# S5 rotations and input matrices in the down projection's buffers, z split in round 5, eight temporaries, a new order table

## The chip, the cores and the metric

The kernel runs on one core of one Trainium2 chip. The metric is device time in microseconds of one launch. The kernel before takes 1371.43 us, the median of three runs (1370.65 to 1372.84).

## The reference, cut to what matters

One layer of a hybrid decoder, for 1024 prompt positions and 8 x 4 sample positions, which stand side by side as 1056 columns (NT). All is float32.

```
proj   = x @ w_in                          # x_lru | u_s5 | two gates
h_lru  = rg_lru(conv4(x_lru))              # gated linear recurrence, 1024 channels
y_s5   = s5_ssm(u_s5)                      # complex diagonal state space, 32 groups of 16 channels, 64 states
z      = gelu(y_s5);  glu = z @ w_glu
merged = sigmoid(g_lru) * h_lru + sigmoid(g_s5) * glu_a * sigmoid(glu_b)
x1     = layer_norm(ALPHA * x + merged @ w_out)
up     = x1 @ w_up                         # 2 x 3072
f      = (gelu(conv3(up_a)) * up_b) @ w_down
y      = layer_norm(ALPHA * x1 + f)
```

The states after the last position are returned too.

## The kernel before, in words

Each large product is taken in three passes. A float32 tensor is split into a high part (rounded by ScalarE, `scopy`) and the rest (subtracted on VectorE, `tt`); TensorE adds hi*hi, hi*lo and lo*hi in PSUM. So each weight tile costs one load (`wx`), one ScalarE cast (`wh`) and one VectorE subtraction (`wl`), all of 128x1024.

The program has these stages. First come four tiles of the input projection for S5 (PSUM tiles `psu`), with the parameters of S5 worked out beside them in a long chain of small VectorE operations (`s5_params`, line 705). Then eight rounds j follow (line 1104). A round has three products of 72 matmuls of 352 columns each: the RG-LRU input (`psx`), the RG-LRU gate (`psl`) and the S5 gate (`psg`); then the recurrence of one block of 128 channels (`lru_rec`), whose two gate products are six small groups of three matmuls (`psr`). Beside them, S5 runs in four batches ut: `s5_consts(ut)` (step c, line 809) makes the batch's tables and `s5_batch(ut)` (step b, line 881) runs it; `z_split` (step z, line 1075) splits the result for the next product. PLAN says in which round each of these stands in the written program. The GLU product (`psab`), the output projection (`pso`) with the first layer norm, the up projection (`ps`) and the down projection (`pd`) with the second layer norm follow. The last two use a scheme of seven products in place of eight, which needs sums of weight tiles: `s_prep(q)` (line 1409) loads four tiles of w_down (`spx`, `spy`, `spz`, `spv`), forms four sums on VectorE and stores them to DRAM (`s`) for the down projection, for q from 0 to 5.

In S5 the names are: `par` holds the parameters, `tmc` products of them, `CA` the output matrices, `bk` the input vectors laid out for a product `psk`, `BA` and its transpose `BT` (through PSUM, `pst`) the input matrices, `F` the rotations, `U` the input, `V` its image (`psv`), `G` the scanned states, `H` the states turned back, `psy` the output, and `zs` its place in DRAM.

Buffers are rings: a tile takes the slot that comes free first, and its first writer waits for that. The ring "w" has ten slots of 1024 numbers for weights; in the kernel before it also serves `F` and `BT` (INW, line 306). The ring "p" has three slots (NPREP, line 242); in the kernel before its users are `s_prep` and later the input pieces of the down projection. The ring "e" has seven temporaries, "m" six small ones.

The order is set by a planner that runs when the program is built (`schedule`, line 144). Each recorded operation has a priority: its place in the written program less the sum of the boosts of its labels (DEFAULT and BOOST). The planner steps through time with a cost for each operation, and gives an engine the ready operation of the best priority among those that could start soonest. The tiles of one ring are taken in the order of the written program. All loads and stores are issued by SyncE, one after another. Each engine then runs its own list in order on the chip; an instruction that waits holds back all that stand behind it on its engine.

Of the kernel before, what the change touches and what calls it, by code (L numbers as in the profile page):

```python
# [8 lines left out]
F32 = mybir.dt.float32  # L9
# [60 lines left out]
class Program:  # L70
# [173 lines left out]
SPREP = {4: 0, 7: 1, 10: 2, 13: 3, 16: 4, 19: 5}  # L244
NWT_SLOT = 10
LOOK = 2
NSLOT, NTEMP, NMID = 28, 7, 6
PE1 = [0, 0, 0, 1]
PE2 = [0, 4, 0, 0]
SPL = (1,)  # L250
BACC = {"dynamic_dma_scratch_size": 1024}
PLAN = {0: "c0 b0 c1", 1: "b1 c2", 2: "b2 c3", 3: "b3", 4: "z0 z1 z2 z3"}
DEFAULT = {"df": 200, "dw": 200, "l": -100, "w": 300, "wa": 300, "wu": 300, "s": 200, "e": 150}
BOOST = {
# [34 lines left out]
}  # L289
WCUT = [slice(0, 256), slice(256, 512), slice(512, 1024)]  # L290
XCUT = 2
# [11 lines left out]
LACT = 'b'  # L303
G1 = [2, 2, 2, 2]
G2 = [4, 1, 4, 4]
INW = {"F", "BT"}


def build(tc, ins, outs):
# [103 lines left out]
    with ExitStack() as st_:  # L413
# [6 lines left out]
        def slot(shape, dt=F32, name="sl"):  # L420
            return pr.tile(up, shape, dt, "u", NSLOT, name)
# [10 lines left out]
        def wslot(shape, dt=F32, name="wt"):  # L432
            return pr.tile(wp, shape, dt, "w", NWT_SLOT, name)
# [3 lines left out]

        def sslot(shape, name):
            key = name.rstrip("0123456789")
            return wslot(shape, F32, name) if key in INW else slot(shape, F32, name)  # L440

        def fixed(shape, name, dt=F32):
            return pr.tile(cp, shape, dt, name, 1, name)
# [213 lines left out]
        par = slot([1088], name="par")  # L657
# [309 lines left out]
        def lru_in(j):  # L967
            psx = mmps(f"psx{j}")
            gemm(psx, wtile(lgpos(0, j)), xs)
            xp = temp([1083], name=f"xp{j}")  # L970
            gset(xp[:, 0:3], 0.0)
            xq = xp[:, 1027:1083].rearrange("p (b q) -> p b q", q=7)
            with boosted("e"), boosted("ex"):
                for c in range(NCH):
                    n = CH if c < 2 else 320
                    scopy(xp[:, 3 + CH * c:3 + CH * c + n], psx[c][:, :n])
                scopy(xq[:, :, 3:7], psx[2][:, 320:352].rearrange("p (b q) -> p b q", q=4))
            gcopy(xq[:, :, 0:3], lh[:, j])
            gcopy(olru[:, j, 0:3], xp[:, 1024:1027])
            gcopy(olru[:, j, 3:27].rearrange("p (b q) -> p b q", b=NB), xq[:, :, 4:7])  # L980
            xc = temp([LL], name=f"xc{j}")
            with boosted(f"cv{j}"):
                act(xc[:, :], xp[:, 3:3 + LL], AF.Identity, bias=cv("cb")[:, j:j + 1], scale=cw[:, 3, j:j + 1])
                for k in range(3):
                    stt(xc[:, :], xp[:, k:k + LL], cw[:, k, j:j + 1], xc[:, :], MUL, ADD)
            return xc

        def lru_gate(j):
            psl = mmps(f"psl{j}")
            gemm(psl, wtile(lgpos(1, j)), xs)  # L990
            gg = temp([NT], name=f"gg{j}")
            with boosted("e"), boosted("egl"):
                for c in range(NCH):
                    act(gg[:, CH * c:CH * c + CH], psl[c][:, :CH], AF.Sigmoid)
            return gg
# [102 lines left out]
        u_tile(3)  # L1098
        cs = {}
        plan = PLAN  # L1100
        cur = lru_in(0), lru_gate(0)
        if GWPOS == 0:
            lru_weights(0)
        for j in range(NK):
            nxt = None
            if GWPOS == 1:
                lru_weights(j)
            if j + 1 < NK:
                if GWPOS == 0:
                    lru_weights(j + 1)  # L1110
                with boosted(f"in{j + 1}"):
                    xc = lru_in(j + 1)
                with boosted(f"lg{j + 1}"):
                    nxt = xc, lru_gate(j + 1)
            with boosted(f"gs{j}"):
                s5_gate(j)
            for w in plan.get(j, "").split():
                q = int(w[1])
                with boosted(f"s{j}"), boosted(w):
                    if w[0] == "c":  # L1120
                        cs[q] = s5_consts(q)
                    elif w[0] == "b":
                        s5_batch(q, cs.pop(q))
                    else:
                        z_split(q)
            if GWPOS == 2:
                lru_weights(j)
            lru_rec(j, *cur)
            cur = nxt
        dma(outs["o_lru"], olru)  # L1130
        dma(outs["o_s5"], os5)
# [537 lines left out]
```

## Time and profile before

| what | before |
|---|---|
| median of three runs | 1371.43 us |
| the profiled execution's own time | 1372.17 us |
| its span | 1370.4 us |
| TensorE matmul busy | 1332.7 us |
| VectorE busy | 1084.0 us |
| ScalarE busy | 599.3 us |
| granted TensorE clock, mean | 0.99 |

The span runs from the first to the last instruction of the profiled execution; the launch's own time is 1.8 us longer. A matmul's record overlaps that of the next, so a busy TensorE says only that it never stood still; how fast it went is read from the number of matmuls in a stretch and the time of that stretch. "Idle before" names who released the engine.

### The profile page before, as it was taken

What the parts mean: (1) busy time and instruction counts of PE and PEld (TensorE: products, weight loads), DVE (VectorE), ACT (ScalarE), POOL (GpSimd) and SP (SyncE); (2) the same over time, 40 slices, a digit from 0 to 9 for tenths busy, and PEclk for the clock granted to TensorE, in tenths of its full rate; (3) what the DMA queues carried; (4) which work ended last, traced back from release to release, by engine and by line L of the source; (5) the groups of instructions that cost most, each with busy time, mean ns of one, the idle gap of its engine ahead of it and who ended that gap; (6) DMA issues with size and microseconds to landing.
All of it is one profiled execution on the core that took longest, in us unless ns stands there. A gap on an engine that the chain in (4) does not pass through costs nothing.

```text
span 1370.4 us, 24666 instructions
## 1 busy us (share of the span) xinstructions
PE 1332.7 (97%) x10040; PEld 1319.6 (96%) x10040; DVE 1084.0 (79%) x1825; ACT 599.3 (44%) x800; POOL 70.2 (5%) x184
## 2 busy tenths in 40 slices
PE   8999988999999999999999999999999999999995
PEld 8999888899999999999999999999999999999995
DVE  6989998896589865779999788888788875555895
ACT  6422625657678332455333333333332443433463
POOL 0000011010011000000010000000000000000000
PEclk9999998999999999999999999999999999999997
DMA  9856744434223651142343322332222387864251
GB/s 333 270 173 228 220 139 110 105 100 153 77 79 127 239 191 47 65 126 93 105 137 127 118 94 103 110 110 87 94 102 87 133 318 292 307 204 158 65 204 64
DMA packets 89330, 201.88 MB, mean 147 GB/s; under 512 B 11008, under 2 KB 40832, under 8 KB 89216
## 3 DMA queue, kind: packets, MB, share of 16 engines
q1 hardware_dynamic: 89216, 200.30, 43.7%
q8 instruction: 79, 1.29, 0.4%
q14 instruction: 35, 0.29, 0.1%
HBM read 142.17 MB, written 58.09 MB: 146 GB/s over the span
## 4 chain that ended last, share of the span: by engine, by line
PE 87%; DVE 7%; issue 2%; ACT 1%; DMA 1%; SPq 1%; DVEq 0%; ACTq 0%
PE ps L395 35%; PE pd L395 18%; PE pso L395 7%; PE psab L395 7%; PE psg L395 5%; PE psl L395 4%; PE psx L395 4%; PE psu L395 4%; PE psr L395 2%; DVE tmc L327 1%; DVE tm L327 1%; SPq L374 1%; DVE xc L339 1%; PE psy L395 1%; DMA wx<-wall 1%
## 5 line engine op out<-in xcount | busy, mean ns | idle before, releaser
L395 PE MATMUL pd<-fh,dh 128*128 128x264 f32 x672 | 192.3, 286 | 0.0
L395 PE MATMUL pd<-fh,dl 128*128 128x264 f32 x672 | 191.3, 285 | 0.0
L395 PE MATMUL pd<-fl,dh 128*128 128x264 f32 x672 | 190.9, 284 | 0.0
L395 PEld LDWEIGHTS pd<-fl,dh 128*128 128x128 f32 x672 | 126.5, 188 | 0.2
L395 PEld LDWEIGHTS pd<-fh,dh 128*128 128x128 f32 x672 | 126.4, 188 | 0.2
L395 PEld LDWEIGHTS pd<-fh,dl 128*128 128x128 f32 x672 | 126.6, 188 | 0.0
L327 DVE TENSOR_TENSOR dl<-dx,dh 128x1024 fp32r<-128x1024 f32 x48 | 58.1, 1220 | 48.8 <-ACT dh L364 44.2
L395 PE MATMUL pso<-mm,wh 128*128 128x264 f32 x512 | 95.4, 287 | 0.0
L364 ACT CAST dh<-dx 128x1024 fp32r<-128x1024 f32 x48 | 49.8, 1049 | 81.0 <-PE pd L395 71.3
L339 DVE SCALAR_TENSOR_TENSOR ac<-fx,con,ac 128x1072 f32<-128x1072 f32 x48 | 64.0, 1333 | 25.9 <-ACT ac L360 25.3
L395 PEld LDWEIGHTS pso<-mm,wh 128*128 128x128 f32 x512 | 79.9, 188 | 0.5
L364 ACT CAST wsh<-wa 128x1024 fp32r<-128x1024 f32 x24 | 25.2, 1051 | 122.7 <-DVE wa L327 113.2
L395 PE MATMUL pso<-mm,wl 128*128 128x264 f32 x256 | 72.7, 284 | 0.0
L327 DVE TENSOR_TENSOR wl<-wx,wh 128x1024 fp32r<-128x1024 f32 (+2 forms) x48 | 54.1, 1130 | 16.7 <-ACT wh L364 10.5
L395 PE MATMUL psg<-xh,wh 128*128 128x352 f32 x192 | 63.8, 332 | 3.5 <-ACT wh L364 3.5
L395 PE MATMUL psg<-xh,wl 128*128 128x352 f32 x192 | 63.2, 329 | 1.5 <-DVE wl L327 1.5
L364 ACT CAST wh<-wx 128x1024 fp32r<-128x1024 f32 (+2 forms) x48 | 46.8, 976 | 40.8 <-DMA wx<-wall 34.8
L395 PE MATMUL psab<-zh,wl 128*128 128x352 f32 (+1 forms) x200 | 63.4, 317 | 0.0
L395 PE MATMUL psab<-zh,wh 128*128 128x352 f32 (+1 forms) x200 | 63.4, 317 | 0.0
L395 PE MATMUL psab<-zl,wh 128*128 128x352 f32 (+1 forms) x200 | 63.1, 316 | 0.0
L395 PE MATMUL psg<-xl,wh 128*128 128x352 f32 x192 | 63.1, 328 | 0.0
L395 PE MATMUL psl<-xh,wh 128*128 128x352 f32 x192 | 62.6, 326 | 0.0
(321 smaller groups left out, 4570.0 us busy)
## 6 DMA issues: line engine op xcount, KB each, us to landing
f<-gt SPq DMA_DIRECT2D x84, 264.0 KB, 2.1
wx<-wall SPq DMA_DIRECT2D x42, 512.0 KB, 4.6
fr<-f SPq DMA_DIRECT2D x30, 528.0 KB, 5.5
wa<-wall SPq DMA_DIRECT2D x29, 512.0 KB, 4.4
wg<-wall SPq DMA_DIRECT2D x24, 512.0 KB, 3.6
dx<-wall SPq DMA_DIRECT2D x24, 512.0 KB, 4.4
dx<-s SPq DMA_DIRECT2D x24, 512.0 KB, 6.3
fr<-f SPq DMA_DIRECT2D x24, 264.0 KB, 3.3
```

The costliest lines, as they stand in the source:

```text
L327: pr.add("DVE", 69 + 1.0417 * fsize(out), lambda: V.tensor_tensor(out=out, in0=a, in1=b, op=op), [a, b], [out])
L339: lambda: V.scalar_tensor_tensor(out=out, in0=a, scalar=sc, in1=b, op0=op0, op1=op1),
L364: pr.add("ACT", (51 if psum(a) else 93) + 0.8333 * fsize(out), lambda: S.copy(out, a), [a], [out])
L374: pr.add("SP", fsize(x) * x.ap[0][1] * 4 / 320.0, lambda: nc.sync.dma_start(out, a), [a], [out])
L395: T.matmul(o, lhsT=l, rhs=r, start=st, stop=sp, skip_group_check=skip)
```

## The change

`F` and `BT` are now taken from the ring "p" by `prep` (INP). In the written program S5 stands ahead of `s_prep`, so "p" now serves the eight tiles of S5 first, then the 24 of `s_prep`, then the down projection's input pieces. The ring "w" holds weights alone. There are eight temporaries in place of seven and five small ones in place of six. The four z splits stand in round 5 of the plan, not 4. The whole table of boosts is new. A new function `s5_steps` holds the loop over a round's S5 steps; a plan may now name steps behind the recurrence (after a "|"), but this plan has none.

```
-NSLOT, NTEMP, NMID = 28, 7, 6
+NSLOT, NTEMP, NMID = 28, 8, 5
-PLAN = {0: "c0 b0 c1", 1: "b1 c2", 2: "b2 c3", 3: "b3", 4: "z0 z1 z2 z3"}
+PLAN = {0: "c0 b0 c1", 1: "b1 c2", 2: "b2 c3", 3: "b3", 5: "z0 z1 z2 z3"}
 BOOST = {
...
-    "gs4": 31, "gs5": 3401, "gs7": 68, "in2": 499, "in3": 128, "in4": 1996, "in5": -36, "in7": -11, "l20": 1043,
...
+    "s3": 5923, "s4": 61, "s5": 564, "sp0": -1857, "sp1": 1911, "sp2": 105, "sp4": 297, "sp5": 55, "ue0": 18,
...
-INW = {"F", "BT"}
+INW = set()
+INP = {"F", "BT"}
...
         def sslot(shape, name):
             key = name.rstrip("0123456789")
-            return wslot(shape, F32, name) if key in INW else slot(shape, F32, name)
+            return (wslot if key in INW else slot)(shape, F32, name) if key not in INP else prep(shape, name)
...
+        def s5_steps(steps, j):
+            for w in steps.split():
+                q = int(w[1])
+                with boosted(f"s{j}"), boosted(w):
+                    if w[0] == "c":
+                        cs[q] = s5_consts(q)
+                    elif w[0] == "b":
+                        s5_batch(q, cs.pop(q))
+                    else:
+                        z_split(q)
...
-            for w in plan.get(j, "").split():
...
+            before, _, after = plan.get(j, "").partition("|")
+            s5_steps(before, j)
             if GWPOS == 2:
                 lru_weights(j)
             lru_rec(j, *cur)
+            s5_steps(after, j)
             cur = nxt
```

What the new table does to the order is shown at three places; the names end in the tiles' own numbers.

SyncE near the start, before: the first DMAs behind the load of the third weight tile (`wx_149`); `scs` is the block of S5 parameters.

```order
L374 DMA wx_149<-wall 128x1024
L374 DMA spx_1028<-wall 128x1024
L374 DMA spy_1029<-wall 128x1024
L374 DMA spz_1030<-wall 128x1024
L374 DMA wgx_181<-wgate 128x256
L374 DMA scs<-scon 128x1072
L374 DMA sbc<-scon 128x1024
```

The same place of the kernel after:

```order
L375 DMA wx_149<-wall 128x1024
L375 DMA wgx_184<-wgate 128x256
L375 DMA scs<-scon 128x1072
L375 DMA sbc<-scon 128x1024
L375 DMA wx_152<-wall 128x1024
L375 DMA wx_155<-wall 128x1024
```

The loads of `s_prep` have left this place. The first of them now stands behind the loads of the fourth batch's tables, two rows ahead of a weight tile of round 6 (`wx_480`), and the last of the 24 stores just ahead of the loads for the first layer norm.

VectorE where S5's first tables are made, before: from the first `CA` to the last `bk` of batch 0.

```order
L327 TENSOR_TENSOR CA_210<-tmc_209 64x512 x2
L339 SCALAR_TENSOR_TENSOR xc_173<-xp_172,con,xc_173 128x1080
L327 TENSOR_TENSOR tmc_209<-sbc,par 128x512 x2
L339 SCALAR_TENSOR_TENSOR CA_210<-tmc_209 64x512 x2
...
L327 TENSOR_TENSOR wl_192<-wx_190,wh_191 128x1024
L327 TENSOR_TENSOR tb<-sbc,tmp 128x256
L327 TENSOR_TENSOR spv_1116<-spv_1116,spz_1115 128x1024
L327 TENSOR_TENSOR par<-tb 128x256
L327 TENSOR_TENSOR wl_200<-wx_198,wh_199 128x1024
L343 COPY bk_211<-par 64x4x16 x2
```

The same place of the kernel after:

```order
L328 TENSOR_TENSOR CA_210<-tmc_209 64x512 x2
L328 TENSOR_TENSOR tb<-sbc,tmp 128x256
L328 TENSOR_TENSOR tmc_209<-sbc,par 128x512 x2
L328 TENSOR_TENSOR par<-tb 128x256
L340 SCALAR_TENSOR_TENSOR CA_210<-tmc_209 64x512 x2
L344 COPY bk_211<-par 64x4x16 x2
L328 TENSOR_TENSOR tmc_209<-par 128x512
```

The `spv` sum, the weights' subtractions and the three convolution steps `xc` have left the stretch. On TensorE the product that needs `CA` and `bk`, `psk_212`, has moved with them: before it stood behind the second of the three parts of round 1's `psx`, after 480 matmuls; now it stands straight behind round 0's `psx`, after 360.

TensorE at the first recurrence (`psr`), before: one row of each group is shown.

```order
L395 MATMUL psr_0_0_248<-xch_245,wgh_182 128x360
...
L395 MATMUL psr_0_1_249<-xch_245,wgh_182 128x360
...
L395 MATMUL psr_0_2_250<-xch_245,wgh_182 128x360
...
L395 MATMUL psr_1_0_252<-xch_245,wgh_182 128x360
...
L395 MATMUL psr_1_1_253<-xch_245,wgh_182 128x360
...
L395 MATMUL psg_0_276<-xh_80,wh_265 128x352
```

The same place of the kernel after:

```order
L396 MATMUL psr_0_1_249<-xch_245,wgh_182 128x360
...
L396 MATMUL psx_0_261<-xh_80,wh_199 128x352
...
L396 MATMUL psr_0_2_250<-xch_245,wgh_182 128x360
...
L396 MATMUL psr_1_0_252<-xch_245,wgh_182 128x360
...
L396 MATMUL psx_1_262<-xh_80,wh_199 128x352
...
L396 MATMUL psr_1_1_253<-xch_245,wgh_182 128x360
```

The six groups stood one behind another; now 24 matmuls of a wide product stand between each two pairs. The recurrences of rounds 1 and 2 were taken apart in the same way. From the output projection on, TensorE's list is the same but for a few swaps of neighbouring groups, and its last 60 rows are the same row for row.

## Rows read from the trace of the kernel before

**Rows 1.** The page: span; busy us (share) and instructions of two engines.
```profile
span 1370.4 us, 24666 instructions
...
PE 1332.7 (97%) x10040; PEld 1319.6 (96%) x10040; DVE 1084.0 (79%) x1825; ACT 599.3 (44%) x800; POOL 70.2 (5%) x184
```

**Rows 2.** Busy time by stretch: from:to, length, engines, granted clock, DMA share, GB/s.
```profile
100.00:200.00 100.00, 95.85 (x670) 92.47 (x669) 94.76 (x158) 38.50 (x63) 8.76 (x21) 1.00 0.62 199
200.00:250.00 50.00, 42.92 (x269) 39.85 (x265) 44.53 (x80) 26.67 (x38) 6.00 (x12) 0.86 0.35 87
...
280.00:400.00 120.00, 120.00 (x757) 120.00 (x756) 81.70 (x94) 76.93 (x102) 11.25 (x20) 1.00 0.32 103
400.00:510.00 110.00, 110.00 (x708) 110.00 (x708) 90.35 (x107) 61.36 (x90) 8.59 (x9) 1.00 0.54 178
...
660.00:1285.00 625.00, 625.00 (x5126) 624.92 (x5125) 483.72 (x783) 221.10 (x244) 26.25 (x88) 1.00 0.42 147
```

**Rows 3.** The chain that ended last: start us, us, what.
```profile
54.78 11.57 PE psx L395 x72
...
204.70 0.64 PE pst L399 x4
...
252.47 1.85 PE psk L395 x29
...
274.38 1.08 PE psv L395 x16
...
298.81 2.78 PE psy L395 x24
...
359.46 1.00 PE psr L395 x6
...
412.66 1.92 PE psab L395 x12
...
434.95 75.44 PE psab L395 x492
510.40 26.27 PE pso L395 x216
```

**Rows 4.** The same chain inside 200 to 280 us.
```profile
207.88 3.21 PE psr L395 x9
...
217.59 6.10 PE psg L395 x22
...
264.80 0.77 PE psr L395 x3
265.60 0.57 ACT gt L360
```

**Rows 5.** VectorE from 50 to 280 us by form: count, busy us, mean ns.
```profile
L327 DVE TENSOR_TENSOR wl<-wx,wh 128x1024 fp32r<-128x1024 f32 x14 | 17.0, 1217 | 5.1 <-ACT wh L364 5.1
...
L327 DVE TENSOR_TENSOR spz<-spy,spz 128x1024 f32<-128x1024 f32 x5 | 6.1, 1219 | 0.0
```

**Rows 6.** VectorE's timeline from 54 to 90 us: start, us, instruction.
```profile
56.26 1.22 DVE L327 TENSOR_TENSOR spy<-spx,spy 128x1024 f32<-128x1024 f32 x1
...
66.04 1.28 DVE L327 TENSOR_TENSOR tmc<-sbc,par 128x512 f32<-128x512 f32 x2
...
69.83 1.34 DVE L339 SCALAR_TENSOR_TENSOR xc<-xp,con,xc 128x1080 f32<-128x1080 f32 x1
71.09 1.28 DVE L327 TENSOR_TENSOR tmc<-sbc,par 128x512 f32<-128x512 f32 x2
...
82.49 1.23 DVE L327 TENSOR_TENSOR wl<-wx,wh 128x1024 fp32r<-128x1024 f32 x1 [3.06 <-ACT wh L364]
...
85.89 0.41 DVE L343 COPY bk<-par 64x64 f32<-64x64 f32 x2
```

**Rows 7.** ScalarE's timeline from 30 to 42 us: the sines of S5.
```profile
38.08 0.32 ACT L360 ACTIVATE tmp<-tmp 128x16 f32<-128x16 f32 x2
```

**Rows 8.** TensorE's waits over the span: waited for, us in total, times, longest.
```profile
PE psg L395 <- ACT wh L364: 3.5, 2, 3.2
...
PE ps L395 <- ACT fx L364: 1.4, 1, 1.4
```

More of the change, by code (lines that the diff above doesn't have):

```diff
@@ L1116, in build @@
                 s5_gate(j)
-            for w in plan.get(j, "").split():
[L1118 to L1125, printed above, removed]
+            before, _, after = plan.get(j, "").partition("|")
+            s5_steps(before, j)
             if GWPOS == 2:
```

66 rows, old and new, of the table BOOST are left out of this document.

## Prediction

> **What bounds the kernel now.** I read the page's first part, then busy time by stretch, then the chain that ended last, then VectorE's forms and timeline. By the page TensorE is busy 1332.7 of 1370.4 us [rows 1]. From 660 to 1285 us, and from 280 to 510, it never stands still [rows 2], so whatever is gained ahead of 280 us is handed on whole, as long as nothing else falls late. The place to look at is 50 to 280 us, where TensorE has gaps and VectorE is busy 94.76 us of 100 [rows 2].
>
> What TensorE loses there I take by counting its work from the first `psx` to the first `pso`, that is from 54.78 to 510.40 us, 455.6 us [rows 3], at the pace of undisturbed pieces. Eight rounds of three products of 72 matmuls at 11.57 us are 277.7. The 144 `psr` at 1.00/6 us are 24.0. Of 600 `psab` 492 take 75.44, and the other 108 at 1.92/12 take 17.3. S5's float32 matmuls show as two records each: 128 `psk` at 1.85/29 us (8.2), 128 `psv` at 1.08/16 (8.6), 128 `psy` at 2.78/24 (14.8); with 32 transposes at 0.64/4 (5.1) the sum is 431.1 us [rows 3]. So 24.5 us are lost, all of it ahead of 280 us. Part of it is the clock: nine `psr` took 3.21 us where 1.50 are due, and 22 `psg` 6.10 where 3.5 are due, 4.3 us together [rows 4]; the mean granted clock of that stretch is 0.86 [rows 2], so the engine ran part of it at 1.2 GHz and the rest at 2.4, after waits around the transposes at 204.70 and the `psr` at 207.88 us [rows 3, 4]. Part is the six `psr` groups in a row: three matmuls take 0.77 us, then a ScalarE step of 0.57 us must free one of two PSUM banks [rows 4]. The largest named wait, 3.2 us of `psg` for a cast [rows 8], is also of this stretch. The rest is waiting for S5's tables.
>
> **The sums of `s_prep` leave the front.** Of the 24 sums 20 run between 50 and 280 us: four forms of five, 6.1 us each, 24.4 us [rows 5]. None feeds anything before the down projection. They go because `F` and `BT` hold "p" until S5 is through. The planner had put them into short pauses of chains; on the chip a sum of 1.22 us in a pause of some tenths pushes the chain back by most of its length. Started behind one another such operations cost 1.14 us (1.22 less the 0.08 by which the records of two neighbours overlap, as 69.83 and 71.09 show for an operation of 1.34 [rows 6]). Taken whole that is 22.8 us of VectorE time that the front no longer carries, against 24.5 us lost: of the right size, but not one for one, because the order of TensorE changes too.
>
> **S5 starts earlier, and waits at its start.** `psk` of batch 0 stands 120 matmuls earlier, so TensorE reaches it at 54.78 + 11.57 = 66.4 us. When is VectorE ready? Before, 28.0 us pass from the sines (38.08) to the first `tmc` (66.04) [rows 6, 7]. Four sums lie in it (the `spy` at 56.26 is one), 4.6 us; without them 23.4 remain, and as many weight subtractions stand there as before. The sines come at most 1 us sooner: S5's parameters no longer queue behind 1.5 MB of `s_prep` on SyncE, but the sines stand behind copies of `psu` on ScalarE, which TensorE sets. That gives 60.5 us. From the first `tmc` to the last `bk` 20.3 us pass before [rows 6]; three `xc` at 1.26, three weight subtractions and one sum at 1.14 and the wait of 3.06 us leave the stretch, 11.4 us, so 8.9 remain: 69.4 us. TensorE waits 3 us. The next such place is `pst`: 2.0 us of `psk` and 48 matmuls (7.7) later, at 79.1 us, it needs `BA`, which VectorE has after three `xc`, one subtraction, four operations like `tmc`, and small ones, about 11 us, so at 80.4 and for the second half 2 us later than TensorE could use it: 2 us. By the same count `psy` of batch 0 just fits, `psk` of batch 1 waits 1.3 us, and I leave 2 us for what I can't see: 8.3 in all. From there VectorE is ahead: with its list priced by the means of its forms and TensorE's by its pace, the tables of batches 1 and 2 stand 7 to 37 us further ahead of their users than before. Queued behind the wait at `psk` on TensorE are `psl` of round 0 and all else, so the wait counts in full. Bounds: if the chain from the sines does not shorten, 5 us more; if VectorE's list runs without pauses, all but 2 us vanish. I keep 2 to 14 and take 8.
>
> **The `psr` groups are taken apart.** With 24 matmuls (3.9 us) between pairs, 0.57 us of ScalarE is covered; if the cover is gone, 0.7 us a group comes back, 8 us for batches 0 to 2 at most. This and the clock are inside the 24.5 us.
>
> **What comes later.** The 20 sums, their 20 loads and 20 stores go to 280 to 510 us, where VectorE is busy 81.70 + 90.35 = 172 us of 230 [rows 2]: with 24.4 us it is at 85%. Batch 3 also moves 169 rows back on TensorE (27 us), so some 13 us of its VectorE work falls here too: 91%. Loads and stores, 20 MB, add 90 GB/s to 103 and 178; at 0.54 of the DMA engines for 178 GB/s this reaches 0.8. I cost it at nothing, covered by the 9% and by DMA queues that are not full; the bound is the second rival. The z splits a round later, the small ring at five and 51 table loads on ScalarE where 46 stood (76.93 us of 120 busy) have room. The ring "w" with all ten slots lets weights come earlier, which is in the vanishing 3.2 us wait. The start and the tail don't change: the first loads carry the same bytes ahead of the first matmul, and the last TensorE rows are the same. The 1.4 us at `ps` [rows 8] I leave.
>
> **Sum.** 24.5 - 8 = 16.5 us gained. From the profiled execution's own 1372.2 us that is 1355.7; the median of the runs lies 0.7 lower, so 1355 us.
>
> **Rivals.** First, the clock. The waits at 66 and 79 us lie among float32 `psk` and transposes, as the waits before the slow stretch did [rows 3, 4]. If the clock falls again, 4.3 us come back by [rows 4]: 1359. The Trainium skill, TensorE: Matmul & The Clock Gate, section on a second failure mode, says that short idles between groups that cycle through PSUM banks can swing the clock between its levels. This trace agrees at 200 to 250 us, and shows full clock in 100 to 200 us despite 4.2 us without matmuls [rows 2], so I give it 13%.
>
> Second, slower. VectorE falls late between 400 and 510 us. At 91% the stretch is as dense as 100 to 200 us was, and a sum whose load is late holds all behind it, the merges (`mm`) too, for which `pso` waits. If the loss per us is that of before (24.5 us in 230), the same 24.5 us are lost again, and with the 8 us at the start the kernel stands at 1372 + 8 = 1380. It decides from the point at which VectorE's pauses exceed 9% there. For it speaks that the last sum stands only 16 operations ahead of the last merge in VectorE's list; against it that at 82% (90.35 of 110 us) TensorE lost nothing there [rows 2]. 11%.
>
> Third, nothing. The loss was S5's own latency, not VectorE's load, and comes back in the new order at other places: 1369. The Trainium skill, Perfetto Trace Analysis, on identifying the most-contended engine, would name TensorE by the whole run, and then a change that takes no matmul away gives nothing; its passage on several regimes in one kernel says the opposite, and the stretches of [rows 2] show two regimes. 12%.
>
> **How the numbers follow.** The forecast (gain 10 to 23 us) has 61%, the clock 13%, nothing 12% (half within 0.2%, which is 2.7 us and about what a measurement of this kernel can tell), slower 11%, and 3% for more than 23 us. The likeliest case alone spans 1349 to 1362. For 8 in 10 I take 1345, which is nearly all of the loss and the 1.4 us regained, to 1368. Faster 0.83, same 0.06, slower 0.11.
>
> **What would show it.** In the profile after, the first `pso` should start near 494 us, not 510. TensorE's waits should name `psk` for `bk` and `pst` for `BA` with 2 to 4 us each between 66 and 82 us, and little from 120 to 280. No sum should stand ahead of 280 us, the granted clock of 200 to 250 us should be 1.00, and `psr` should wait for no `gt`. I am wrong if TensorE loses over 3 us between 280 and 510 us, or if the waits ahead of 120 us exceed 14 us.

## The result and the profile after

The kernel after takes 1353.03 us, the median of four runs (1352.81 to 1353.98); the kernel before took 1372.13 us beside it (1370.65 to 1373.48). The ratio is 0.986, with a 95% interval of 0.9845 to 0.9879, a gain of 19 us. Forecast were 1355 us and a range of 1345 to 1368.

The page of the kernel after answers to [rows 1]:

```profile
span 1351.0 us, 24674 instructions
...
PE 1326.4 (98%) x10040; PEld 1318.4 (98%) x10040; DVE 1080.8 (80%) x1825; ACT 603.9 (45%) x805; POOL 79.8 (6%) x184
```

The work is the same. TensorE's busy time is only 6 us less, which says little, since a matmul's record overlaps that of the next. The stretches of [rows 2] in the kernel after (columns as there; its last stretch ends 19 us sooner):

```profile
100.00:200.00 100.00, 100.00 (x702) 98.78 (x701) 78.39 (x134) 49.37 (x73) 10.21 (x23) 1.00 0.36 92
200.00:250.00 50.00, 49.29 (x330) 48.17 (x329) 39.23 (x64) 26.72 (x38) 5.60 (x11) 1.00 0.20 65
280.00:400.00 120.00, 118.90 (x764) 118.05 (x765) 103.02 (x115) 81.02 (x108) 21.83 (x20) 1.00 0.73 245
400.00:510.00 110.00, 110.00 (x740) 110.00 (x739) 100.49 (x128) 58.55 (x86) 8.19 (x9) 1.00 0.76 254
660.00:1266.00 606.00, 606.00 (x4969) 605.93 (x4968) 464.95 (x750) 214.48 (x238) 24.47 (x84) 1.00 0.43 149
```

From 200 to 250 us 330 matmul records stand where 269 stood, and the clock is 1.00, not 0.86. VectorE falls from 94.76 to 78.39 us of 100 in the front, and rises from 172 to 203.5 us of 230 behind it. The last stretch is full in both.

Where the time went is read from two starts. The `psx` and `pso` products of the kernel after (instruction form and count; shortest, median, longest ns; first and last start in us):

```profile
L396 PE MATMUL psx<-xh,wh x192: 317/323/431, 54.9 to 354.5; 128*128 128x352 f32 x192
L396 PE MATMUL pso<-mm,wh x512: 278/284/483, 492.0 to 589.4; 128*128 128x264 f32 x171
```

From the first to the other 437.1 us pass, where 455.6 passed before [rows 3]: 18.5 of the 19 us are gained between them. TensorE's waits in the kernel after from 54 to 520 us are few (us in total, times, longest):

```profile
PE psk L396 <- DVE bk L344: 2.0, 1, 2.0
PE psv L396 <- ACT V L365: 1.6, 2, 1.1
PE psv L396 <- issue: 0.2, 1, 0.2
```

The 3.5 us of `psg` for `wh` [rows 8] are gone, and no wait of `psr` or `pst` is listed. The 1.4 us of `ps` for `fx` [rows 8], behind this stretch, are gone too. The chain that ended last shows the start of S5 in the kernel after (start, us, what):

```profile
59.97 1.17 DVE tmc L328 x2
...
68.27 0.20 DVE bk L344
...
68.60 2.25 PE psk L396 x29
70.85 9.09 PE psl L396 x48
79.94 0.87 PE pst L400 x8
```

`tmc` stood at 66.04 us before, and the last `bk` at 85.89 [rows 6]. The 48 `psl` take 9.09 us where 7.7 are due (48/72 of 11.57), and the 29 `psk` 2.25 where 1.85 are due [rows 3], because the clock falls behind the wait for `bk`. The granted clock is the third number from the end of a stretch's row; from 70 to 74 us it is 0.58:

```profile
70.00:74.00 4.00, 4.00 (x24) 3.94 (x20) 3.90 (x11) 2.48 (x3) 0.45 (x3) 0.58 0.01 3
```

All 24 sums now run between 299 and 479 us. One of their four forms in the kernel after, from 280 to 510 us, as in [rows 5]:

```profile
L328 DVE TENSOR_TENSOR spz<-spy,spz 128x1024 f32<-128x1024 f32 x6 | 7.3, 1216 | 0.1
```

### The profile page after: what moved, and what is told of

It reads as the page before. It is cut to its first block, busy times and chain, and to the rows that moved or that the text cites. A ratio compares the mean times of both kernels' runs of the same rounds, so it can differ in the third digit from the quotient of the medians.

```text
span 1351.0 us, 24674 instructions
## 1 busy us (share of the span) xinstructions
PE 1326.4 (98%) x10040; PEld 1318.4 (98%) x10040; DVE 1080.8 (80%) x1825; ACT 603.9 (45%) x805; POOL 79.8 (6%) x184
## 4 chain that ended last, share of the span: by engine, by line
PE 93%; DVE 3%; ACT 2%; DMA 1%; issue 1%; SPq 0%; ACTq 0%; DVEq 0%
PE ps L396 36%; PE pd L396 18%; PE pso L396 7%; PE psab L396 7%; PE psg L396 7%; PE psl L396 6%; PE psx L396 5%; PE psu L396 2%; PE psr L396 1%; PE psy L396 1%; DVE tmp L328 1%; DMA wx<-wall 1%; PE psk L396 1%; PE psv L396 0%; DVE par L328 0%
## 5 line engine op out<-in xcount | busy, mean ns | idle before, releaser
L340 DVE SCALAR_TENSOR_TENSOR ac<-fx,con,ac 128x1072 f32<-128x1072 f32 x48 | 64.0, 1333 | 24.5 <-ACT ac L361 23.7
L365 ACT CAST wh<-wx 128x1024 fp32r<-128x1024 f32 (+2 forms) x48 | 47.1, 982 | 38.0 <-DMA wx<-wall 23.6
L361 ACT ACTIVATE ac<-fx,con 128x1072 f32<-128x1072 f32 x24 | 30.8, 1285 | 74.4 <-DVE fx L328 65.4
L396 PE MATMUL psl<-xl,wh 128*128 128x352 f32 x192 | 62.5, 326 | 0.0
```

The source lines that it names most:

```text
L340: lambda: V.scalar_tensor_tensor(out=out, in0=a, scalar=sc, in1=b, op0=op0, op1=op1),
L361: pr.add("ACT", c, lambda: S.activation(out=out, in_=a, func=f, bias=bias, scale=scale), [a] + [x for x in (bias, scale) if isap(x)], [out ...
L365: pr.add("ACT", (51 if psum(a) else 93) + 0.8333 * fsize(out), lambda: S.copy(out, a), [a], [out])
L396: T.matmul(o, lhsT=l, rhs=r, start=st, stop=sp, skip_group_check=skip)
```

## The experiments

The theory to test (A) was the prediction's: the sums' VectorE time in the front is the loss. Its rivals were that TensorE's order is what counts (B), and that the new table is (C).

For each kernel the table gives the time that TensorE loses between the first `psx` and the first `pso`. The starts of all its products stand in the trace; from the time to the next start I take what the same product takes undisturbed (the fastest fifth of its kind in the kernel after), and what is left over is lost. Some 5 us of each row are small steps between kinds of products, so the rows are to be compared with each other. The orders differ, so the cut is made by work done and not by time: "front" is the first 210 us of work, which end at 273 us in the kernel after; "behind" is the rest. "To before" is the ratio to the kernel before, run beside it, with its interval.

| kernel | median us | to before | front lost | behind lost |
|---|---|---|---|---|
| before | 1372.1 | | 29.1 | 0.5 |
| after | 1353.0 | 0.9862 (0.9845-0.9879) | 8.1 | 2.8 |
| 1 before, sums late | 1387.3 | 1.0101 (1.0086-1.0116) | 25.8 | 18.9 |
| 2 after, 20 extra operations | 1367.7 | 0.9961 (0.9948-0.9974) | 24.1 | 3.0 |
| 3 before, ring alone | 1400.1 | 1.0195 (1.0180-1.0210) | 8.9 | 48.6 |
| 4 after, ring undone | 1391.7 | 1.0136 (1.0119-1.0153) | 43.4 | 7.4 |
| 5 after, `psr` in a row | 1356.6 | 0.9887 (0.9871-0.9904) | 10.7 | 5.3 |
| 6 after, z in round 4 | 1371.8 | 0.9998 (0.9988-1.0007) | 8.0 | 23.6 |
| 7 before, all but the table | 1386.7 | 1.0108 (1.0092-1.0123) | 10.6 | 34.7 |
| 8 after, three small moves | 1353.8 | 0.9865 (0.9851-0.9880) | 9.5 | 3.5 |
| 9 before, weights early | 1390.5 | 1.0128 (1.0113-1.0143) | 30.7 | 19.6 |
| 10 after, start shifted | 1353.0 | 0.9854 (0.9838-0.9871) | 7.7 | 2.8 |
| 11 after, sizes undone | 1382.9 | 1.0077 (1.0061-1.0093) | 7.7 | 32.8 |
| 12 run 9, one reader early | 1391.0 | 1.0131 (1.0109-1.0154) | 30.3 | 16.7 |

**1. The sums alone.** The order that the planner made is kept, and only `s_prep` is moved in it (the list of places, BEHIND, is left out here).

```
+        order = self.schedule()
+        moved = {i for v in BEHIND.values() for i in v}     # the 72 operations of s_prep
+        for i in order:
+            if i not in moved:
+                for k in (i, *BEHIND.get(i, ())):
+                    self.ops[k][2]()
```

> The kernel before with its own order, sizes, rings and table; only the 72 operations of `s_prep` (24 loads, 24 sums, 24 stores) are taken out of the planned order and put back about where the kernel after has them (none ahead of 280 us). TensorE's list stays the old one: `psk` of batch 0 behind 480 matmuls, `psr` groups in a row. Theory A (the sums' VectorE time in the front is the loss, in whichever order): of the loss ahead of 280 us the waits for S5's tables between 196 and 224 us (about 12 us with the half clock behind them) go, the `psr` groups in a row keep some 6 us: 1354 to 1361 us. Theory B (the loss is TensorE's order: S5's products too late and `psr` in a row; VectorE's time was hidden): 1368 to 1373 us, nothing gained.

VectorE did become free where the sums had stood, up to 193 us. From 100 to 150 us it is busy 35.28 us of 50, where it was 47.50 before. From 200 to 250 us, where no sum stood, it is as busy as before (44.08 against 44.53), and the granted clock is 0.83, no better than the 0.86 of before:

```profile
100.00:150.00 50.00, 49.79 (x360) 48.59 (x359) 35.28 (x75) 15.24 (x29) 1.01 (x6) 1.00 0.21 53
...
200.00:250.00 50.00, 44.24 (x254) 41.24 (x254) 44.08 (x78) 26.06 (x38) 6.03 (x13) 0.83 0.31 85
```

The front won 3.3 us of 29.1. TensorE's waits no longer name `bk`, `CA` or `BA`, but the others stayed, and the half clock with them (from 54 to 520 us; of the 3.5 us of `psr` for `gt` 2.1 lie ahead of 280 us):

```profile
PE psr L409 <- ACT gt L374: 3.5, 8, 0.9
PE psg L409 <- ACT wh L378: 3.2, 2, 3.0
...
PE pst L413 <- DVE F L357: 1.4, 1, 1.4
PE pst L413 <- ACT xch L378: 1.3, 1, 1.3
```

So theory A falls for the old order: 22.8 us of VectorE's time taken away give 3.3. And with the same 72 operations the stretch behind loses 18.4 us more, where the kernel after loses 2.3 more. Theory B did not foresee that either: it said 1368 to 1373. Which of the waits behind the front the moved operations cause was not taken apart.

**2. VectorE's time alone, in the new order.**

```
         for i in self.schedule():
             self.ops[i][2]()
+            if i in EXTRA:
+                self.extra()
...
+        full = con[:, 0:960].rearrange("p (a b) -> p a b", a=16)
+        pr.extra = lambda: V.tensor_reduce(out=dum[:, :], in_=full, axis=AX.X, op=ADD)
```

> The kernel after with 20 extra VectorE operations of about a sum's length (a reduction of 128x960) put into VectorE's list at the times at which the 20 sums stood before, from 56 to 191 us; nothing waits for them, no DMA goes with them, and TensorE's order is the new one. Theory A (VectorE's time in the front counts): most of 20 x 1.1 = 22 us comes back, 1363 to 1375 us, with TensorE waiting for `bk`, `BA` and the tables of batches 1 and 2. Theory B (the new order of TensorE brought the gain): 1353 to 1357 us.

The extra operations from 50 to 200 us by form (the twentieth starts at 208.0 us), TensorE's waits from 54 to 300 us, and its stretch from 183 to 192 us:

```profile
L472 DVE TENSOR_REDUCE dum<-con 128x16 f32<-128x960 f32 x19 | 21.7, 1142 | 0.0
```

```profile
PE psk L401 <- DVE bk L349: 5.0, 1, 5.0
PE psy L401 <- POOL H L373: 4.9, 2, 3.9
PE psk L401 <- DVE CA L345: 3.1, 2, 2.8
```

```profile
183.00:192.00 9.00, 6.58 (x31) 6.58 (x32) 8.62 (x20) 3.35 (x4) 1.48 (x2) 0.62 0.33 111
```

14.7 us come back for some 22 us of VectorE's time (16.0 in the table's count). 11.0 of these 16.0 us are waits for S5's tables and states, 13.0 in the three rows where the kernel after has 2.0. The other 5 are lower clock behind such waits, as in the last row (0.62). In the new order theory A holds; theory B falls. The two runs together: neither the sums' leaving nor the new order gives the 21 us of the front by itself (3.3 and 5.0 us); together they do. Run 2 does not put back the loads and stores of `s_prep`, so its 5.0 us are the new order's and theirs together.

**3 and 4. The ring alone, and all but the ring.**

```
-INW = {"F", "BT"}
+INW = set()
+INP = {"F", "BT"}
```

> The kernel before with one part of the change alone: `F` and `BT` from the ring p; old table, seven temporaries, six small ones, z split in round 4. The planner then puts all 24 sums behind VectorE's work for S5, `psk` of batch 0 straight behind round 0's `psx`, and a wide product between the `psr` pairs. Theory A (the ring alone is the lever, since it moves the sums; the rest follows from it): 1351 to 1360 us. Theory C (the new table of boosts brings the gain): 1366 us or more.

> The kernel after with that one part undone: `F` and `BT` in the ring w again; new table, eight temporaries, five small ones, z split in round 5. The planner then puts 23 of 24 sums among S5's work again, `psk` of batch 0 behind 72 more matmuls, the `psr` groups of batches 1 and 2 in a row. Theory A: back to 1364 to 1376 us. Theory C (the table): 1353 to 1359 us.

The ring alone makes the whole gain of the front, with the old table: 8.9 us lost, not 29.1. With the ring undone, the new table loses 43.4, more than the old one did, and run 4's 1391.7 us lie above both of its ranges. So the ring is the lever of the front, as theory A says, and the table is not. But the ring alone is 28 us slower than before, because it loses 48.6 us behind the front. TensorE's two long waits from 280 to 520 us in that kernel:

```profile
PE psg L396 <- ACT xp L365: 25.8, 1, 25.8
PE psx L396 <- ACT gg L361: 8.2, 1, 8.2
```

`xp` and `gg` are ScalarE's copies of products into temporaries; until they run, the PSUM banks stay full. Both expectations for run 3 named a time that left this out.

**5. The `psr` groups in rows again.**

```
+    634: [633, 635, 636, 637, 638, 639, 640, 641, 642, 643], 832: [831, 833, ... 841], 1030: [1029, 1031, ... 1039],
```

> The kernel after with the `psr` groups of batches 0, 1 and 2 put back into rows (six, five and five in a row, with their ScalarE readers between them, as in the kernel before); all else in its order. Theory (one ScalarE step of about 0.6 us per group stands open on TensorE when no wide product lies between): about 13 groups by 0.3 to 0.7 us, 4 to 9 us slower, and the half clock perhaps with it: 1357 to 1365 us. Rival (another wait covers it, the row costs nothing by itself): 1352 to 1355 us.

It costs 3.6 us, just under the lower end of the theory. TensorE's waits from 54 to 300 us show little at `psr` itself; most of it moved to the bank of the next `psv`. Its longest wait, near 281 us, is 2.7 us, not 1.1, and now the clock falls behind it (0.66 from 286 to 291 us):

```profile
PE psv L404 <- ACT V L373: 3.5, 2, 2.7
PE psk L404 <- DVE bk L352: 2.0, 1, 2.0
PE psr L404 <- ACT gt L369: 0.7, 4, 0.2
```

```profile
286.00:291.00 5.00, 5.00 (x26) 4.82 (x25) 3.65 (x5) 4.18 (x6) 1.19 (x1) 0.66 0.17 40
```

**6. The z splits in round 4 again.**

```
-PLAN = {0: "c0 b0 c1", 1: "b1 c2", 2: "b2 c3", 3: "b3", 5: "z0 z1 z2 z3"}
+PLAN = {0: "c0 b0 c1", 1: "b1 c2", 2: "b2 c3", 3: "b3", 4: "z0 z1 z2 z3"}
```

> The kernel after with the four z splits in round 4 of the plan again; ring, table and sizes as after. TensorE's list is the same up to the fourth batch's `psy`. Theory from the run with the ring alone (`zh` casts wait in ScalarE's list for `zs`, which the fourth batch now delivers late, and the copies of `psx`, `psl` and `psg` behind them hold TensorE): 10 to 40 us slower, 1363 to 1393 us, the loss between 290 and 400 us. Rival (the prediction's: the z split a round later has room either way): 1351 to 1356 us.

18.8 us slower, which is nearly all of the gain, in one wait. The chain that ended last in that kernel shows its end, TensorE's waits from 280 to 400 us name it, and ScalarE's timeline has the copy:

```profile
344.82 2.06 DVE zl L328 x2
...
346.90 0.46 ACT xp L365
...
347.40 2.72 PE psg L396 x8
```

```profile
PE psg L396 <- ACT xp L365: 18.6, 1, 18.6
```

```profile
346.90 1.23 ACT L365 COPY xp<-psx 128x352 f32<-128x352 f32 x4 [0.94 <-DVE zl L328]
```

A split takes a temporary for `z` until VectorE has made `zl`. `xp` takes the next one of the same ring, so it waits for `zl`; `psg` waits for the bank that `xp` empties. In round 4 the splits stand ahead of that `xp` in the ring's order. The chip's own wait for `zl` is only the last 0.94 us. The rest is the place of the copy in ScalarE's list: the planner takes the ring's tiles in order, and put it behind the casts of three splits and behind an `av` that waits 3.60 us for VectorE. In the kernel after these copies follow their products, the first at 303.14 us, and no split stands ahead of them. The expectation saw the list and not the ring that made it.

**7. All but the table.** Run 3 with z in round 5, eight temporaries and five small ones.

> The kernel before with all of the change but the new table: `F` and `BT` in the ring p, z split in round 5, eight temporaries, five small ones, old boosts. Theory (the ring makes the front, the z split's place guards the stretch behind it, the table only trims): of the 45 us that the ring alone lost between 297 and 372 us some 35 go: 1356 to 1372 us. Rival (the table is needed to place the 72 operations of `s_prep` and the z splits): 1380 us or more.

The stretch behind loses 34.7 us, 14 fewer than with the ring alone, not 35 fewer. The waits from 330 to 490 us are again an `xp`, and now a weight's second part late on VectorE, in whose list recurrences, merges and sums stand close together:

```profile
PE psg L396 <- ACT xp L365: 13.6, 1, 13.6
PE psab L396 <- DVE wl L328: 11.2, 1, 11.2
```

VectorE's timeline of that kernel shows the second: from 463.57 to 478.02 us it has no break, and the weight stands at the end of it.

```profile
473.20 1.21 DVE L328 TENSOR_TENSOR spv<-spv,spz 128x1024 f32<-128x1024 f32 x1
...
476.81 1.21 DVE L328 TENSOR_TENSOR wl<-wx,wh 128x1024 fp32r<-128x1024 f32 x1
```

The theory that the table only trims falls: it is worth 33.7 us here (1386.7 against 1353.0), all of it behind the front but 2.5.

**8 and 10. Towards a faster kernel.** Run 8 moves three operations of TensorE's list; run 10 moves three wide products ahead by one place among batch 0's small ones (the order's places, by operation number).

```
run 8    +    401: [463], 1067: [921], 1115: [1228],
run 10   +    385: [401], 402: [403], 490: [416],
```

> A version meant to beat both: the kernel after with three operations of TensorE's list moved by one wide product of 24 matmuls each (`psk` of batch 0 behind the first `psl`; the fourth `psv` of batch 2 behind the next `psx`; the third `psl` of round 5 ahead of the third `psv` of batch 3). Theory (TensorE waits 2.1 us for `bk`, 0.7 and 1.2 us for a PSUM bank; the half clock of 1.3 us follows the first wait): 3.5 to 5.5 us faster than after, 1347 to 1350 us. Rival (the waits only move to the next step of the same chains): 1351 to 1354 us.

> The kernel after with three wide products of 24 matmuls moved ahead by one place among batch 0's small ones: the first `psl` ahead of `psk`, the third ahead of `pst`, the first `psx` of round 1 ahead of `psv`. In the run with `psk` alone moved, the wait went to `pst` (1.7 us) and the half clock to the stretch around it. Theory (both waits are covered, `psv` stands at its old time): 1.5 to 3.5 us faster than after, 1349.5 to 1351.5 us. Rival (the last tables of batch 0 come when VectorE has them, and the wait goes on to `psy`): 1352 to 1354 us.

Both take the same time as the kernel after. In run 8 the wait for `bk` became waits of `pst` and `psy`; in run 10 it became waits of `psy` and a later `psk`. Rows of run 8 from 54 to 500 us, then of run 10 from 54 to 300 us:

```profile
PE psy L403 <- DVE tm L335: 1.5, 1, 1.5
PE pst L407 <- DVE tb L335: 1.5, 1, 1.5
```

```profile
PE psy L403 <- POOL H L375: 1.6, 1, 1.6
...
PE psk L403 <- DVE CA L347: 1.0, 2, 0.7
```

In both the rival held: batch 0's chain on VectorE (and the `H` on GpSimd) ends when it ends, and the reordering of TensorE only chooses where some 2 to 5 us are waited. No version here beats the kernel after.

**9 and 12. Why did the old order lose time at 200 us, if not by the sums?** In the kernel before SyncE issues no weight load for 41 us; its queue's rows there:

```profile
165.02 0.38 SPq L374 DMA_DIRECT2D wx<-wall  x1
...
206.23 0.42 SPq L374 DMA_DIRECT2D wx<-wall  x1
```

In the kernel after there are three in that time (at 168.60, 186.37 and 197.92 us). Runs 9 and 12 start from run 1, keep its order with `F` and `BT` in the ring p, and bring two weight tiles forward, with the three products of one of them; run 12 also moves one reader of a `psr` bank.

```
run 9    +    696: [865], 875: [866], 742: [867, 883], 891: [884], 779: [885], 762: [895], 807: [896], 832: [897],
run 12   +    839: [841],
```

> The kernel of the first run (the order of before, the 72 operations of `s_prep` late; 1387 us), but `F` and `BT` stand in the ring p while the order stays the one planned for the ring w, and the slots that this frees are used for two weight tiles alone: load, cast and subtraction of the tiles of round 2's `psg` and round 4's `psx` stand some 30 to 40 us earlier, and the three `psg` products are put between `psy`, `psk`, `pst` and `psr` of batches 1 and 2. Theory (in the kernel before TensorE has no wide product at hand from 193 to 217 us, since `F` and `BT` hold the slots of the ring w and no weight is loaded from 165 to 206 us): of about 17 us lost there 8 to 14 go, 1373 to 1380 us. Rival (the loss there is the small products' own latency and the half clock): 1384 to 1388 us.

> The kernel of the ninth run (1390.5 us) with one ScalarE operation moved: the reader `gt` of batch 1's sixth `psr` stands straight behind that of the fifth, not behind the gate's `av`, `th` and table loads. In the ninth run the `psv` of batch 2 waited 7.0 us for the PSUM bank that this reader frees, and `psy` of batch 2 5.9 us for VectorE's states behind it. Theory (the kernel before loses its time around 200 us by the order of small steps: no weight at hand, and a bank's reader late on ScalarE): both waits go but for 1 to 2 us, and 10 to 14 us with them: 1376 to 1381 us. Rival (S5's chain on VectorE sets the time of `psy` whatever stands ahead): the first wait goes, the second grows: 1384 to 1390 us.

Both theories of mine failed, and both runs lie above their rivals' ranges too. The second 70 us of work did win 7 us in run 9 (12.1 lost in run 1, 5.0 here), but the third lost 12 more. TensorE's waits from 140 to 280 us in run 9, and from 140 to 290 us in run 12:

```profile
PE psv L410 <- ACT gt L375: 7.0, 1, 7.0
PE psy L410 <- DVE tm L342: 5.9, 1, 5.9
```

```profile
PE psv L410 <- ACT V L379: 8.6, 3, 7.2
PE psy L410 <- DVE tm L342: 4.3, 1, 4.3
```

With the weights there, `psv` waits for a bank whose reader stands behind the gate's `av` and `th` on ScalarE; with that reader moved, for the next reader, which stands there too. So the old order is held up by neither of these two alone. S5's batch 2 and the gate of batch 1 come at the same time there, and my reading, which no run tests, is that each step waits for the last.

## Why the prediction was right, and where it was not

**The time, and where it shows: right.** The first `pso` starts at 492.0 us (forecast 494), the clock from 200 to 250 us is 1.00, no sum stands ahead of 280 us, and no `psr` wait is listed. TensorE lost 2.8 us in all behind the front (1.1 of it at the `psv` near 281 us), under the 3 that were set as the bound. That the sum came within 2 us is in part luck, as the next paragraph shows.

**The loss at the start: the right place, too large.** The first `tmc` was forecast for 60.5 us and the last `bk` for 69.4; they stand at 59.97 and 68.27. Of the 8.3 us of waits the 2.0 at `psk` came (3 forecast). Neither `pst` nor `psk` of batch 1 waited: `pst` starts at 79.94, after `psk` and `psl` had been slowed by the clock, and run 8 shows that where `psk` does not wait, `pst` does (1.5 us and 0.7 us). The half clock cost 1.8 us more (1.4 on `psl`, 0.4 on `psk`), which stood in the rival and not in the sum. So 3.8 us were lost at the start, not 8. By the prediction's own count of 431.1 us of work, the 437.1 us of the kernel after leave 6.0 lost: these 3.8, and 2.2 behind the front, for which the sum had nothing. The two misses, 4.2 and 2.2 us, partly cancel, and what is left is the 2 us by which the forecast is too high.

**The clock.** The rival with the lower clock came true in part: one stretch at 0.58 behind the wait at `psk`, 1.8 us of the 4.3 that were set for it. Run 10 covers that wait, and there the clock is 1.00 from 66 to 90 us:

```profile
66.00:90.00 24.00, 23.98 (x190) 23.02 (x189) 23.09 (x68) 9.52 (x17) 1.75 (x7) 1.00 0.26 72
```

**"The sums of `s_prep` leave the front", 22.8 us against 24.5 lost: the step that failed as a cause.** The two numbers agreed, and I took the agreement for the mechanism, with no more than the reserve that it would not be one for one. Run 1 takes this time away, with the order kept, and wins 3.3 us in the front. What runs 1 to 4 show in its place: the ring does two things at once. It sends the sums away, and with it the planner, which then has a free VectorE and free weight slots, lays S5 out 120 matmuls earlier with wide products between the small ones. Without the second the free VectorE time stays idle (35.28 us busy of 50 from 100 to 150 us in run 1); without the first the new order waits for its tables (14.7 us in run 2). How much of the second is due to the weight slots and how much to VectorE's room in the plan is not settled: sums ahead of 280 us in the real kernel with the slots free could not be had, as both use the same three buffers, and runs 9 and 12, which gave the old order its weights, won nothing.

**"The `psr` groups are taken apart": right in kind.** The cover was priced at 8 us at most; run 5 measures 3.6 us.

**"What comes later: at nothing": nearly the right sum, for a wrong reason.** Some 2 us more than before were lost there. The text named VectorE's idle 9% and the DMA queues as the cover, and gave the z splits, the small ring and the table loads "room". The loads were near the forecast (VectorE busy 203.5 of 230 us, 88% and not 91%; DMA share 0.73 to 0.76, not 0.8), but idle time covers nothing by itself: with the same operations to place, z in round 4 loses 21 us more there, the old sizes 30 more, and the old table 32 more. All three are parts of the change that keep the loss there near nothing. Run 11 takes the sizes alone:

```
-NSLOT, NTEMP, NMID = 28, 8, 5
+NSLOT, NTEMP, NMID = 28, 7, 6
```

> The kernel after with seven temporaries and six small ones again, the rest as after; TensorE's list ahead of 260 us is the same. Theory (the z splits and the merges need the eighth temporary, since a split holds one until its second part is subtracted): 3 to 20 us slower, 1356 to 1373 us, lost between 300 and 480 us. Rival (the prediction's: the sizes have room): 1352 to 1355 us.

It measured 1382.9 us, beyond the theory's upper end. TensorE's waits from 280 to 480 us in that kernel:

```profile
PE psx L396 <- ACT gg L361: 7.7, 1, 7.7
PE psab L396 <- ACT sb L361: 7.7, 2, 6.4
PE psg L396 <- ACT xp L365: 6.4, 1, 6.4
```

All three are ScalarE's copies into temporaries of the same ring. The planner laid the stretch out anew for the sizes, so the 30 us are those of seven temporaries, of six small ones and of this plan together.

**The slower rival** put its price on VectorE falling late between 400 and 510 us. Losses of that size exist (runs 3, 6, 7 and 11), but most of them lie earlier, between 290 and 440 us, and what is late there is a temporary. The rival as it was written was met once, in run 7, with the 11.2 us of `psab`; the new table avoids it. **"Nothing", S5's own latency**, is what runs 8 and 10 show for the last 2 us, and what runs 9 and 12 met in the old order; that it is hidden in the kernel after because S5 starts earlier is my reading.

## What to carry to other kernels

When a sum of removed work equals the time lost beside it, that is not yet the cause: take the work away with the order kept, and put it back with the order changed, before believing it. In a kernel laid out by a planner, moving two kinds of tiles to another ring changes the plan, and most of the gain and of the danger lies there; each of the "small" edits beside it (a step a round later, one more temporary) can be worth the whole gain. A stretch in which VectorE is 88% busy is safe or not by what its in-order queues wait for, above all by which tile of a ring comes next, and not by its idle share.

## What was not expected of the hardware

A wait of 2.0 us on TensorE beside small float32 products was followed by a granted clock of 0.58 from 70 to 74 us, though TensorE had been busy without a break from the first `psx` at 54.9 us to that wait; the 1.1 us that `psv` waited for a bank near 281 us were not followed by one (1.00 from 280 to 400 us), but the 2.7 us of the same wait in run 5 were (0.66 from 286 to 291 us). Taking the first wait away took the dip away (run 10), though not the lost time.
